# Two-block transformer on one core: the running sums of squares and of the layer norms made by VectorE, not by GpSimd

## The chip, the core and the metric

The kernel runs on one core of a Trainium2 chip. The metric is device time in microseconds (us) of one execution; three runs of the kernel before gave 1494.23, 1493.85 and 1490.75, a median of 1493.85. TensorE (PE) multiplies matrices, VectorE (DVE) and ScalarE (ACT) work elementwise, GpSimd (POOL) does a few elementwise operations here, and SyncE (SP) issues most DMAs. The activations live in SBUF, the products in PSUM; POOL reads and writes SBUF only.

## The reference, cut to what matters

Batch 1, model width D = 1024, 272 tokens (16 meta tokens and 256 of the input). Everything is float32.

```python
def first_block(...):          # two layers
    for i in range(DEPTH):
        a_in = rms_norm(hs, norm_w[i, 0])
        mix = gated_deltanet(a_in, ...) if i % 2 == 0 else mlstm(a_in, ...)
        hs = hs + keep * rms_norm(mix, norm_w[i, 1])
        f = conv_ffn(rms_norm(hs, norm_w[i, 2]), ...)
        hs = hs + keep * rms_norm(f, norm_w[i, 3])
def layer_norm(x, g, b):
    mu = xf.mean(-1, keepdims=True)
    var = jnp.mean(jnp.square(xf - mu), -1, keepdims=True)
    return (xf - mu) * lax.rsqrt(var + LN_EPS) * g + b
def second_block(...):         # two layers: even (convolution, window attention), odd (gated linear, latent attention)
    for layer in range(DEPTH):
        ...
        x = layer_norm(ALPHA * x + y, ln_mix_g[layer], ln_mix_b[layer])
        x = layer_norm(ALPHA * x + swiglu(x, ...), ln_ffn_g[layer], ln_ffn_b[layer])
```

Eight norms close a mixer or a feed-forward: four root-mean-square norms, which need the sum of squares over the width for each token, and four layer norms, which need that and the plain sum.

## The kernel before

The width lies on the partitions: a tile of 128 features by 272 (later 258 or 256) tokens, eight tiles m = 0..7 for the model width. Every product is made of three float32r matmuls, from a high and a low part of each operand (`mm3`, lines 350 to 352; side by side in `group`, lines 373 to 376). The weights stream in chunks of eight 128x128 blocks: SP loads `wraw` (line 318), ACT rounds it to `wh` (line 326), DVE makes the rest `wl` (line 327). There are 413 such chunks.

A sum over the width is taken in two steps. Tiles are added up elementwise into one accumulator tile, and TensorE then sums that tile over the partitions with a matrix of ones. The elementwise adds are what this case is about:

- `post_norm` (line 530) closes the mixers and feed-forwards of the first block and is called four times. Its first loop (lines 540 to 546) takes the eight products of the output projection, squares each on ACT (`sq`, line 543) and adds tiles 0 to 6 up in `acc_sq` (lines 442 to 445): six adds. Its second loop (lines 560 to 574) makes, for each tile m, the scaled product `xn` (line 562, DVE, one input in PSUM), the residual `hs` (line 564, DVE, both inputs in SBUF), a square on ACT (line 572), the high part `xh` on ACT (line 568), the low part `xl` on DVE (line 569, both inputs in SBUF), and again six adds of squares (line 573). The last call has no second sum. `pre_norm` and `group` of the next stage multiply `xh` and `xl` with the first weights as they come; the norm's factor is applied later. Below, the stretches of the first three second loops are called residual stage 1 (at 335 us), 2 (548 us) and 3 (690 us).
- `layer_norm` (line 1216) closes the four sublayers of the second block. It adds tiles 0 to 3 into `ac` (line 1257), sums them on TensorE, subtracts that part of the mean (lines 1269, 1271), then adds tiles 4 to 6 into `ac` (line 1263) and the squares of tiles 0 to 6 into `ac2` (line 1249). Behind the product of tile 7 TensorE sums `ac` and `ac2` (lines 1275, 1276, recorded as line 422) and tile 7 and its square (lines 1282, 1283), and goes on with the raw input `xr` of the next stage (line 1242 on DVE, lines 373 to 376 on TensorE). Below, these are layer norms 1 (at 966 us), 2 (1160 us), 3 (1282 us) and 4 (1440 us, the last). In 1 and 3 a product has K = 8, in 2 and 4 K = 22.

In the trace `ac` and `ac2` are both called `lnacc`, and X and the residual both `hs`.

The order of each engine's instructions is not the order of the code. `IssueOrder` (line 1699) takes all instructions, gives each a fixed duration by engine and shape, and schedules them forwards and backwards in turn over their dependencies; `fix` (line 2024) then holds each engine to the order found. For the adds of this case two of its lines count, with n the elements per partition:

```python
        elif e == DVE:
            t = n * 1.042 + 68 + (60 if len(ins) == 3 else 0)
...
        else:
            t = n * 2.25 + 125
```

The second is POOL's. A duration does not depend on what other engines do at that time.

Of the kernel before, what the change touches and what calls it, by code (L numbers as in the profile page):

```python
# [13 lines left out]
D = 1024  # L14
# [18 lines left out]
# ---------------------------------------------------------------- host layout  # L33
# [40 lines left out]
# the order of the first mixer: projections q (with k), v and z, products and blocks P, inverses D, token-major values and keys T, states S, outputs O  # L74
# [65 lines left out]
def host(inp):  # L140
# [34 lines left out]
    # second block, even layer: head t of kv 0 beside head 4 + t of kv 1  # L175
# [10 lines left out]
    # odd layer  # L186
# [72 lines left out]
# ---------------------------------------------------------------- device  # L259
class Kern:  # L260
# [8 lines left out]
    # ---- helpers  # L269
# [40 lines left out]
    def wload(self, first, need, ahead):  # L310
        """Chunks of weights up to `need`, and `ahead` more as far as the buffers behind `first` go."""
# [27 lines left out]
    def wrow(self):  # L339
        """The next four parts side by side."""  # L340
        ci, j = divmod(self.wpos, CH)
        assert j + 4 <= CH
        for _ in range(4):
            self.wnext()
        return [a[:, j:j + 4].rearrange("p a b -> p (a b)") for a in self.wchunks[ci]]
# [16 lines left out]
    def group(self, items, hook=None):  # L362
        """Several products of K = 8 side by side, so that each part of x serves all of them as it comes."""
# [19 lines left out]
    def halves(self, x, n):  # L383
        """The first four products of K = 16: the last part of x is taken last."""
# [23 lines left out]
    def warm(self, k, ins=None):  # L408
        """Products that nothing reads, behind `ins`, so that the array's clock stays up over a wait."""
# [9 lines left out]
    def stat_cols(self, st, src, n):  # L419
        """Sums over the partitions, one column for each 128 tokens (the last ones overlap)."""  # L420
        for i, s in enumerate(starts(n)):
            r = self.nc.tensor.matmul(st[:, i:i + 1], src[:, s:s + 128], self.ones1, start=True, stop=True)
        return r

    def bcast(self, out, col, n):
        """A column for each 128 tokens to rows on all partitions."""
# [7 lines left out]
    def row_stat(self, acc, sq, n, warm=0):  # L434
        """Sum of squares over all tiles: the running sum and the last tile."""
# [6 lines left out]
    def acc_sq(self, acc, prev, sq, m):  # L442
        """Running sum of the squares of all tiles but the last."""
        if m and m < KD - 1:
            self.nc.gpsimd.tensor_tensor(acc, prev if m == 1 else acc, sq, ALU.add)
# [13 lines left out]
    def rstd(self, st, n, dim, pool, tag="rsy"):  # L459
        """1 / sqrt(st / dim + 1e-6), the same rows on all partitions."""  # L460
# [16 lines left out]
    # ---- norms of the first block  # L477
# [5 lines left out]
    def first_raw(self, pool):  # L483
        """The input of the first mixer, not yet normed, and the columns of its sums of squares."""
# [24 lines left out]
    def pre_norm(self, wname, t0, pool, items, outs, dest=None, st=None, tag="rsy"):  # L509
        """The first products of a stage from its input before the norm, scaled after; then the normed input."""  # L510
# [19 lines left out]
    def post_norm(self, wname, K, x, t0, pool, nxt, tag='mix'):  # L530
        """Output projection, its norm, the residual; then the input of the next stage, not yet normed."""
# [46 lines left out]
    # ---- feed-forward with convolution  # L578
# [38 lines left out]
    # ---- gated delta rule  # L617
    def gdn(self):
# [5 lines left out]
        with ExitStack() as es:  # L624
# [17 lines left out]
            # gates  # L642
# [45 lines left out]
            # cumulative sums and last values  # L688
# [13 lines left out]
            # decay matrices, [j, i]: exponents are the sums of g over j < t <= i  # L702
# [77 lines left out]
    def gdn_blocks(self, g, kq, kq16, E, beta, elg, pool, dpool):  # L780
        """Norms of k, scaled products (attention over E) and the inverses of the diagonal blocks of 16."""
# [9 lines left out]
        # the meta tokens, four heads in slots of 32  # L791
# [3 lines left out]
        # products of keys with keys; the squared norms of the keys on their diagonals  # L795
# [27 lines left out]
        # decayed  # L823
# [3 lines left out]
        # the diagonal blocks of 16, one on a partition  # L827
# [5 lines left out]
        # their inverses by substitution  # L833
# [10 lines left out]
        # products of keys with queries  # L844
# [11 lines left out]
    def gdn_inverse(self, g, X64, Uf, st, pool):  # L856
        """The inverse of the triangular matrix, transposed."""
# [6 lines left out]
        # doubling: blocks of 32, 64 and 128  # L864
# [60 lines left out]
    def gdn_tokens(self, g, kq, v, kq16, v16, st, pool):  # L925
        """Values and keys with the tokens on the partitions, scaled."""
# [29 lines left out]
    def gdn_state(self, g, kq, st, neg, egl, pool):  # L956
        """The states before each chunk; the new values of each chunk take the place of the values."""
# [48 lines left out]
    def gdn_out(self, g, kq, E, st, eg, of, pool):  # L1006
        """The outputs, normed and gated, in place of the gates."""
# [12 lines left out]
        # squared norms of q, one column for each token  # L1020
# [16 lines left out]
        for c in (2, 0, 1):  # L1037
# [16 lines left out]
            # head norm  # L1054
# [21 lines left out]
    # ---- mLSTM  # L1076
# [135 lines left out]
    # ---- second block  # L1212
# [3 lines left out]
    def layer_norm(self, name, K, x, pool, last=False, tags=("xr0", "xr1", "xr2", "xr3")):  # L1216
# [11 lines left out]
        if not last:  # L1228
            # the input of the next stage, not yet normed; beside it the gain and the offset as columns
# [14 lines left out]
        def square(m):  # L1244
# [3 lines left out]
            if 1 <= m < KD - 1:  # L1248
                GP.tensor_tensor(ac2, prev if m == 1 else ac2, sq, add)
            prev = sq  # L1250

        for m in range(KD):
            ps = self.proj(K, x, n)
            if m < 4:
                V.scalar_tensor_tensor(X[:, m], X[:, m], ALPHA, ps, mult, add)
                if m:
                    GP.tensor_tensor(ac, X[:, 0] if m == 1 else ac, X[:, m], add)
            else:
# [3 lines left out]
                if 4 < m < KD - 1:  # L1262
                    GP.tensor_tensor(ac, X[:, 4] if m == 5 else ac, X[:, m], add)
# [48 lines left out]
    def norm_product(self, i, raw, pool, out=None, scale=1.0):  # L1312
        """A product of an input before the layer norm: without its offset, and the offset; or all of it."""
# [33 lines left out]
    def softmax(self, pool, sbank, tag, scale, mask, sink, vT, out, tp=None):  # L1347
        """sbank: scores [query, (256 keys of block 1 | 128 keys of block 0)], out: [dv, 256 queries]."""
# [81 lines left out]
    def odd(self, xf):  # L1430
# [5 lines left out]
        with tc.tile_pool(name="op", bufs=1, reuse_waits="tile") as pool:  # L1436
# [18 lines left out]
            # gates of the linear attention, rotary key, queries and keys  # L1455
# [22 lines left out]
            # linear attention: decayed products, level by level  # L1478
# [44 lines left out]
            # latent attention: queries, keys, values  # L1523
# [118 lines left out]
    # ---- whole program  # L1642
# [410 lines left out]
```

## Time and profile before

| | |
|---|---|
| three runs, us | 1490.75, 1493.85, 1494.23 |
| profiled execution: span, us | 1496.2 |
| busy: PE, DVE, ACT, POOL | 97%, 71%, 56%, 13% |
| chain that ended last, by engine | PE 86%, DVE 6%, DMA, POOL and issue 2% each, ACT 1% |
| HBM traffic | 148 GB/s over the span |
| POOL adds of lines 445, 1249, 1257, 1263 | 42, 24, 12 and 8, 86 of POOL's 286 instructions |

The time of the profiled execution is its span, 1496.2 us, 2.4 us over the median of the three runs. A busy share counts an engine as busy while an instruction is on it, also when that runs slowly. The chain that ended last is followed back from the last instruction; PE's share is the time in which it was PE's own work that the end waited for. The granted clock of PE is 1.00 at the higher of its two levels (2.4 GHz) and 0.50 at the lower (1.2 GHz); values between are means over a stretch.

### The profile page before, as it was taken

To read this page: it belongs to the slowest core of one execution; us is meant where nothing else is said; L and a number is where in the kernel's file an instruction comes from. 1 tells how busy PE (TensorE), PEld (TensorE's weight loads), DVE (VectorE), ACT (ScalarE), POOL (GpSimd) and SP (SyncE) were. 2 spreads that over 40 slices of the span, in tenths; PEclk is the share of its full clock that TensorE was granted. 3 is DMA by queue.
4 is the path that set the end of the run, shared out by engine and by line. 5 is a ranking of instruction groups with operands and counts; after the bars stand their busy time and mean duration, and the time that the engine had idled before them with its cause. 6 is when DMAs were issued, how large, how long until landed. Compare 5 with 4: busy or idle time off the path is not lost.

```text
span 1496.2 us, 30607 instructions
## 1 busy us (share of the span) xinstructions
PE 1456.1 (97%) x12258; PEld 1403.7 (94%) x12258; DVE 1056.8 (71%) x1976; ACT 842.9 (56%) x1560; POOL 188.4 (13%) x286
## 2 busy tenths in 40 slices
PE   8899999999999999999999999999999999999997
PEld 7898998998999989889999998999999978999997
DVE  8996585548988357657988456686556798875553
ACT  5456565546766446446766446565444666654442
POOL 3472032121000120003000000020001200300011
PEclk9999998999999999999999999989999999999999
DMA  4343422354655534323665543537555424375551
GB/s 161 103 132 103 150 81 62 112 171 147 215 171 180 172 127 157 119 78 119 206 197 179 189 155 113 176 107 222 187 182 183 144 72 155 128 220 188 182 186 57
DMA packets 72670, 223.96 MB, mean 150 GB/s; under 512 B 16784, under 2 KB 18896, under 8 KB 72400
## 3 DMA queue, kind: packets, MB, share of 16 engines
q1 hardware_dynamic: 71952, 220.38, 45.5%
q8 instruction: 96, 1.57, 0.4%
q10 hardware_dynamic: 576, 1.62, 0.3%
q14 instruction: 46, 0.38, 0.1%
HBM read 220.34 MB, written 1.64 MB: 148 GB/s over the span
## 4 chain that ended last, share of the span: by engine, by line
PE 86%; DVE 6%; DMA 2%; POOL 2%; issue 2%; ACT 1%; SPq 0%; DVEq 0%; ACTq 0%; POOLq 0%
PE acc L352 17%; PE acc L350 17%; PE acc L351 17%; PE psa L350 3%; PE psa L352 3%; PE psa L351 3%; PE psb L351 2%; PE psb L352 2%; PE psb L350 2%; PE acc L376 1%; PE acc L373 1%; PE acc L374 1%; DVE wl L327 1%; POOL Xb L842 1%; DVE hs L564 1%
## 5 line engine op out<-in xcount | busy, mean ns | idle before, releaser
L327 DVE TENSOR_TENSOR wl<-wraw,wh 128x1024 fp32r<-128x1024 f32 x413 | 508.1, 1233 | 228.2 <-ACT wh L326 226.8
L326 ACT ACTIVATE wh<-wraw 128x1024 fp32r<-128x1024 f32 x413 | 435.2, 1056 | 277.8 <-PE acc L351 154.9
L352 PE MATMUL acc<-xh,wl 128*128 128x256 f32 (+1 forms) x848 | 246.7, 291 | 1.2 <-DVE wl L327 1.2
L350 PE MATMUL acc<-xh,wh 128*128 128x256 f32 (+1 forms) x848 | 245.5, 290 | 1.0 <-DVE kq L727 1.0
L351 PE MATMUL acc<-xl,wh 128*128 128x256 f32 (+1 forms) x848 | 245.6, 290 | 0.7 <-issue 0.7
L350 PE MATMUL acc<-ah,wh 128*128 128x256 f32 (+1 forms) x704 | 198.0, 283 | 0.0
L351 PE MATMUL acc<-al,wh 128*128 128x256 f32 (+1 forms) x704 | 197.9, 282 | 0.0
L352 PE MATMUL acc<-ah,wl 128*128 128x256 f32 (+1 forms) x704 | 196.7, 282 | 0.0
L352 PEld LDWEIGHTS acc<-xh,wl 128*128 128x128 f32 x848 | 161.5, 191 | 4.3 <-issue 1.7
L350 PEld LDWEIGHTS acc<-xh,wh 128*128 128x128 f32 x848 | 161.3, 190 | 2.4 <-ACT wh L326 1.2
L351 PEld LDWEIGHTS acc<-xl,wh 128*128 128x128 f32 x848 | 161.1, 190 | 1.5 <-issue 0.9
L350 PEld LDWEIGHTS acc<-ah,wh 128*128 128x128 f32 x704 | 132.5, 189 | 0.1
L351 PEld LDWEIGHTS acc<-al,wh 128*128 128x128 f32 x704 | 132.5, 189 | 0.1
L352 PEld LDWEIGHTS acc<-ah,wl 128*128 128x128 f32 x704 | 131.9, 188 | 0.0
L352 PE MATMUL acc<-xnh,wl 128*128 128x272 f32 (+1 forms) x424 | 122.2, 288 | 0.0
L350 PE MATMUL acc<-xnh,wh 128*128 128x272 f32 (+1 forms) x424 | 122.0, 288 | 0.0
L351 PE MATMUL acc<-xnl,wh 128*128 128x272 f32 (+1 forms) x424 | 121.9, 287 | 0.0
L352 PE MATMUL acc<-oh,wl 128*128 128x256 f32 (+2 forms) x304 | 86.4, 286 | 0.5 <-DVE wl L327 0.5
L351 PE MATMUL acc<-ol,wh 128*128 128x256 f32 (+2 forms) x304 | 86.1, 285 | 0.1
L350 PE MATMUL acc<-oh,wh 128*128 128x256 f32 (+2 forms) x304 | 85.2, 286 | 0.0
L350 PEld LDWEIGHTS acc<-xnh,wh 128*128 128x128 f32 x424 | 79.8, 188 | 1.5 <-issue 1.3
L352 PEld LDWEIGHTS acc<-xnh,wl 128*128 128x128 f32 x424 | 79.8, 188 | 1.4 <-issue 1.2
(715 smaller groups left out, 3483.8 us busy)
## 6 DMA issues: line engine op xcount, KB each, us to landing
wraw<-in_w_dram SPq DMA_DIRECT2D x413, 512.0 KB, 3.4
late<-in_late_dram ACTq DMA_DIRECT2D x1, 1206.5 KB, 5.7
hs<-in_x_dram SPq DMA_DIRECT2D x4, 272.0 KB
out_dram<-hs SPq DMA_DIRECT2D x8, 128.0 KB, 1.9
d<-PT SPq DMA_DIRECT2D x32, 9.0 KB, 1.5
cst<-in_cst_dram SPq DMA_DIRECT2D x1, 339.5 KB
A<-d SPq DMA_DIRECT2D x4, 72.0 KB
d<-Xb SPq DMA_DIRECT2D x4, 72.0 KB
```

Source lines behind the costliest of these rows:

```text
L326: nc.scalar.activation(h, raw, AF.Copy)
L327: nc.vector.tensor_tensor(l, raw, h.bitcast(F32), ALU.subtract)
L350: mm(ps, h, xh, start=start, stop=False)
L351: mm(ps, h, xl, start=False, stop=False)
L352: mm(ps, l, xh, start=False, stop=stop)
L373: mm(o, h, x(k)[0], start=k == 0, stop=False)
L374: mm(o, l, x(k)[0], start=False, stop=False)
L376: mm(o, w[k][0][:, :m], x(k)[1], start=False, stop=k == KD - 1)
L564: V.tensor_tensor(hs, hs, t, ALU.add)
L842: GP.tensor_tensor(Xb[:, j + 1:16, 0:m], Xb[:, j + 1:16, 0:m], tv, sub)
```

## The change

Four lines get another engine. Nothing is added or left out, and the operands stay.

```diff
     def acc_sq(self, acc, prev, sq, m):
         if m and m < KD - 1:
-            self.nc.gpsimd.tensor_tensor(acc, prev if m == 1 else acc, sq, ALU.add)
+            self.nc.vector.tensor_tensor(acc, prev if m == 1 else acc, sq, ALU.add)
...
             if 1 <= m < KD - 1:
-                GP.tensor_tensor(ac2, prev if m == 1 else ac2, sq, add)
+                V.tensor_tensor(ac2, prev if m == 1 else ac2, sq, add)
...
                 if m:
-                    GP.tensor_tensor(ac, X[:, 0] if m == 1 else ac, X[:, m], add)
+                    V.tensor_tensor(ac, X[:, 0] if m == 1 else ac, X[:, m], add)
...
                 if 4 < m < KD - 1:
-                    GP.tensor_tensor(ac, X[:, 4] if m == 5 else ac, X[:, m], add)
+                    V.tensor_tensor(ac, X[:, 4] if m == 5 else ac, X[:, m], add)
```

The diff also drops comments. Since the scheduler knows the engine and the duration of each instruction, it makes a new order for all engines from the first of these adds on (at about 300 us of the trace); before it the order is the same. POOL keeps the small powers (lines 555, 1288) and its part in the first mixer. SP's order is the same.

DVE in layer norm 1, before: from the subtraction of the first part of the mean (lines 1271, 1269) to the first use of the sums (line 1277). `xr` is the low part of the raw input, `wl` a chunk of weights.

```order
L1271 TENSOR_TENSOR hs<-hs,lnpc 128x256 x4
L1269 SCALAR_TENSOR_TENSOR hs<-hs,lnpc 128x256 x3
L1259 TENSOR_TENSOR hs<-hs,acc 128x256
L1269 SCALAR_TENSOR_TENSOR hs<-hs,lnpc 128x256
L1259 TENSOR_TENSOR hs<-hs,acc 128x256
L1242 SCALAR_TENSOR_TENSOR xr<-hs,late,xr 128x256 x4
L327 TENSOR_TENSOR wl<-wraw,wh 128x1024
L1259 TENSOR_TENSOR hs<-hs,acc 128x256
L1242 SCALAR_TENSOR_TENSOR xr<-hs,late,xr 128x256 x2
L327 TENSOR_TENSOR wl<-wraw,wh 128x1024
L1259 TENSOR_TENSOR hs<-hs,acc 128x256
L1277 TENSOR_SCALAR lnp_11941<-psb_11940 128x2
```

The same place in the changed kernel, from tile 5 on. Ahead of these rows stand the eight subtractions, one `xr`, tile 4, another `xr` and three adds of squares.

```order
L1259 TENSOR_TENSOR hs<-hs,acc 128x256
L1249 TENSOR_TENSOR lnacc_11938<-lnacc_11938,lnsq 128x256
L1242 SCALAR_TENSOR_TENSOR xr<-hs,late,xr 128x256
L1263 TENSOR_TENSOR lnacc<-hs 128x256
L1259 TENSOR_TENSOR hs<-hs,acc 128x256
L1249 TENSOR_TENSOR lnacc_11938<-lnacc_11938,lnsq 128x256
L1263 TENSOR_TENSOR lnacc<-lnacc,hs 128x256
L1242 SCALAR_TENSOR_TENSOR xr<-hs,late,xr 128x256
L1249 TENSOR_TENSOR lnacc_11938<-lnacc_11938,lnsq 128x256
L327 TENSOR_TENSOR wl<-wraw,wh 128x1024
L1259 TENSOR_TENSOR hs<-hs,acc 128x256
L1277 TENSOR_SCALAR lnp_11941<-psb_11940 128x2
```

Tile 6 (the third line-1259 row of the kernel before, the second here) and the two sums now stand ahead of the chunk of weights that stood ahead of tile 6, and the fourth `xr` now stands behind the last add into `ac`.

DVE in residual stage 3, before, from the second `xl` to the last ones:

```order
L569 SCALAR_TENSOR_TENSOR xl<-hs,par,xh 128x258
L564 TENSOR_TENSOR hs<-hs,xn 128x258
L562 TENSOR_TENSOR xn<-mix,st 128x258
L564 TENSOR_TENSOR hs<-hs,xn 128x258
L562 TENSOR_TENSOR xn<-mix,st 128x258
L569 SCALAR_TENSOR_TENSOR xl<-hs,par,xh 128x258
L564 TENSOR_TENSOR hs<-hs,xn 128x258
L562 TENSOR_TENSOR xn<-mix,st 128x258
L564 TENSOR_TENSOR hs<-hs,xn 128x258
L569 SCALAR_TENSOR_TENSOR xl<-hs,par,xh 128x258 x5
```

In the changed kernel the first three `xl` stand close together, and the other five behind the last add (`acc`); these are the rows from the fifth `xn` on:

```order
L562 TENSOR_TENSOR xn<-mix,st 128x258 x2
L445 TENSOR_TENSOR acc<-acc,sq 128x258
L564 TENSOR_TENSOR hs<-hs,xn 128x258 x2
L562 TENSOR_TENSOR xn<-mix,st 128x258
L445 TENSOR_TENSOR acc<-acc,sq 128x258
L564 TENSOR_TENSOR hs<-hs,xn 128x258
L562 TENSOR_TENSOR xn<-mix,st 128x258
L445 TENSOR_TENSOR acc<-acc,sq 128x258
L564 TENSOR_TENSOR hs<-hs,xn 128x258
L445 TENSOR_TENSOR acc<-acc,sq 128x258
L569 SCALAR_TENSOR_TENSOR xl<-hs,par,xh 128x258 x4
```

Between the third and the fourth `xl` DVE now has 15 other instructions, where it had three.

## Rows read from the trace of the kernel before

**Rows 1.** The page's first part: busy time, share of the span, instructions.
```profile
PE 1456.1 (97%) x12258; PEld 1403.7 (94%) x12258; DVE 1056.8 (71%) x1976; ACT 842.9 (56%) x1560; POOL 188.4 (13%) x286
```

**Rows 2.** Stretches: length; PE, PEld, DVE, ACT, POOL busy; PEclk, DMA share, GB/s.
```profile
335.00:350.00 15.00, 12.74 (x79) 11.23 (x78) 12.62 (x27) 8.88 (x20) 5.21 (x6) 0.89 0.08 31
...
548.00:562.00 14.00, 12.12 (x92) 10.96 (x93) 12.75 (x28) 8.72 (x19) 5.46 (x7) 1.00 0.12 39
...
690.00:705.00 15.00, 13.11 (x98) 12.19 (x99) 13.64 (x28) 8.38 (x19) 5.25 (x7) 1.00 0.22 70
...
966.00:990.00 24.00, 21.97 (x162) 21.71 (x161) 20.70 (x36) 13.06 (x24) 10.48 (x12) 0.87 0.46 140
990.00:1005.00 15.00, 15.00 (x113) 15.00 (x112) 11.06 (x29) 9.64 (x27) 0.28 (x1) 0.86 0.17 61
...
1285.00:1300.00 15.00, 13.54 (x99) 13.05 (x98) 13.13 (x24) 7.82 (x16) 7.40 (x8) 0.89 0.34 116
```

**Rows 3.** Waits of PE over the span: us in total, times, longest us.
```profile
PE acc L376 <- DVE xl L569: 3.2, 6, 1.3
...
PE psb L422 <- POOL lnacc L1263: 2.6, 2, 2.0
...
PE psa L376 <- DVE xl L569: 1.0, 2, 0.8
...
PE psa L422 <- DVE hs L1259: 0.8, 1, 0.8
```

**Rows 4.** DVE groups, shapes apart: count; busy us, mean ns; idle before.
```profile
L564 DVE TENSOR_TENSOR hs<-hs,xn 128x272 f32<-128x272 f32 x16 | 9.5, 623 | 0.0
L569 DVE SCALAR_TENSOR_TENSOR xl<-hs,par,xh 128x272 fp32r<-128x272 f32 x16 | 8.8, 595 | 0.0
...
L562 DVE TENSOR_TENSOR xn<-mix,st 128x272 f32<-128x272 f32 x16 | 6.4, 429 | 3.3 <-PE st L430 3.3
...
L564 DVE TENSOR_TENSOR hs<-hs,xn 128x256 f32<-128x256 f32 x8 | 3.1, 417 | 0.0
```

**Rows 5.** A POOL group, same columns.
```profile
L445 POOL TENSOR_TENSOR acc<-acc,sq 128x272 f32<-128x272 f32 x20 | 19.0, 951 | 55.2 <-ACT sq L543 51.4 <-ACT sq L572 3.3
```

**Rows 6.** Timeline of DVE in residual stage 1: start us, us; equal neighbours merged (x2).
```profile
335.20 0.78 DVE L562 TENSOR_TENSOR xn<-mix,st 128x272 f32<-128x272 f32 x2 [1.65 <-PE st L430]
335.91 0.79 DVE L564 TENSOR_TENSOR hs<-hs,xn 128x272 f32<-128x272 f32 x2
...
344.91 1.73 DVE L569 SCALAR_TENSOR_TENSOR xl<-hs,par,xh 128x272 fp32r<-128x272 f32 x4
```

**Rows 7.** Timeline of residual stage 3: DVE's first, one `xl`, PE's sum of squares.
```profile
691.33 0.76 DVE L562 TENSOR_TENSOR xn<-mix,st 128x258 f32<-128x258 f32 x2 [0.49 <-PE st L430]
...
693.37 0.49 DVE L569 SCALAR_TENSOR_TENSOR xl<-hs,par,xh 128x258 fp32r<-128x258 f32 x1
...
701.77 0.60 PE L406 MATMUL st<-acc,ones 128*128 128x258 f32 x2
```

**Rows 8.** Timeline of layer norm 1: DVE, POOL and PE at the sums.
```profile
973.51 1.43 DVE L1271 TENSOR_TENSOR hs<-hs,lnpc 128x256 f32<-128x256 f32 x4
...
981.54 1.21 DVE L327 TENSOR_TENSOR wl<-wraw,wh 128x1024 fp32r<-128x1024 f32 x1
982.67 0.41 DVE L1259 TENSOR_TENSOR hs<-hs,acc 128x256 f32<-128x256 f32 x1
...
983.23 0.84 POOL L1263 TENSOR_TENSOR lnacc<-lnacc,hs 128x256 f32<-128x256 f32 x1 [1.89 <-DVE hs L1259]
...
984.12 1.01 PE L422 MATMUL psb<-ones,lnacc 128*128 128x1 f32 x4 [2.03 <-POOL lnacc L1263]
```

**Rows 9.** Stretches of 4 us in layer norm 1, columns as in rows 2.
```profile
960.00:964.00 4.00, 4.00 (x36) 4.00 (x35) 1.71 (x3) 0.53 (x3) 0.00 (x0) 1.00 0.59 194
...
984.00:988.00 4.00, 3.88 (x19) 3.88 (x19) 3.61 (x6) 2.50 (x5) 0.93 (x2) 0.50 0.53 170
```

**Rows 10.** The odd mixer, columns as in rows 2.
```profile
1195.00:1275.00 80.00, 77.41 (x559) 66.63 (x558) 72.19 (x167) 53.51 (x112) 1.62 (x2) 0.96 0.36 117
```

## The prediction

> **What bounds the kernel now.** I began with the page's busy line: PE is at work for 97% of the span, with about 40 us idle in all [rows 1]. So the end is set by PE, and taking 86 adds from POOL and giving them to DVE is worth nothing by itself. What counts is where PE waits, and how fast it runs. The table of waits comes next. Over the whole span PE waits 4.2 us for `xl` of line 569, 2.6 us (twice) for a POOL add of line 1263 and 0.8 us for the `hs` of line 1259 [rows 3]. All of these lie in residual stages and layer norms, where the moved adds are.
>
> Then I cut these places into stretches [rows 2]. In the three residual stages PE is idle for 2.26, 1.88 and 1.89 us, while DVE is busy for 12.62 of 15, 12.75 of 14 and 13.64 of 15: DVE paces them. In stage 1 the mean clock is 0.89, a loss of 15 x 0.11 = 1.65 us. In layer norm 1 it is 0.87 and 0.86 in two stretches on end, although PE does not idle at all in the second. That is the lower level: 19 matmuls in 4 us, against 36 in 4 us twenty microseconds earlier [rows 9].
>
> Last, the shapes one by one show why DVE is so full. The same residual add of line 564 takes 623 ns where POOL adds beside it, and 417 ns, on 256 columns and not 272, in the last `post_norm`, which has no second sum; `xn` of line 562, with one input in PSUM, takes 429 ns in both kinds of company [rows 4]. POOL's adds need 951 ns in the mean [rows 5]. So the adds are not free for DVE today: its instructions with both inputs in SBUF are stretched while POOL works.
>
> **What an add costs on DVE.** No such add runs on DVE before, so I take it from its likes. Two undisturbed line-562 instructions take 0.78 us together, and the next group starts 0.71 us after the first, 0.355 each [rows 6]. Four undisturbed adds of 256 columns take 1.43 us, of which the last has 0.42, so 0.335 each [rows 8]. The low parts `xl` follow each other at (1.73 - 0.49) / 3 = 0.41, where one undisturbed takes 0.49 [rows 6, 7]. The bounds are 0.335 and, if the stretch stayed, 0.62.
>
> **Residual stages.** In stage 1 DVE makes 24 instructions in 335.20 to 346.64, 11.44 us [rows 6]. Afterwards it makes 22 at 0.355 and 8 `xl` at 0.41, 11.1 us. So the six adds (2.1 us) are paid by the stretch that goes: 8 x (0.623 - 0.417) = 1.65 for `hs` and 8 x (0.595 - 0.49) = 0.84 for `xl` [rows 4, 7], 2.5 together. What PE waited longest for here is the fifth `xl` (the first of the last four), done at 345.4; in the new order 21 instructions and five `xl` are done by 335.20 + 7.46 + 2.05 = 344.7. I take 0.5. The slower clock there I leave as it is. Stage 2 has the same counts in an order that suits PE no better: -0.2. In stage 3 the last add ends at 691.33 + 22 x 0.355 + 3 x 0.41 = 700.4, so PE can sum the squares at 700.6 and not at 701.77 [rows 7]. But the fourth `xl` now comes after it, at about the time it had before. I take 1.0 of the 1.2 us. Sum **1.3 us**, between -1.5 (the new order makes PE wait for `xl` in each) and +4 (stage 1 also gets its clock back).
>
> Weighed against this is a rule of the Trainium skill ("Perfetto Trace Analysis", section "Optimizing Scalar/DVE Operations"): where DVE is saturated, offloading some of its work to ScalarE or even GpSimd may make sense. That speaks for the kernel before, since DVE is the full engine in these stages, and by it the stages would lose time. The same passage adds that GpSimd and DVE share a read port of SBUF, so that moving work between those two might not help. The rows with 623 and 417 ns agree with the second sentence, and by that one the stages come out about even, as my sum has it. If only the first held, the second rival below would be the result.
>
> **Layer norm 1.** PE ends its products at about 982.1 and waits 2.03 us for POOL's last `lnacc` [rows 8]. The chain before that is on DVE: tile 6 is drained at 982.67, behind a `wl` of 1.21 us. Afterwards that `wl` stands behind the adds. DVE makes 21 instructions from 973.51 to the last add into `ac`: at 0.335 that is 980.6, and two more bring `ac2` to 981.3, before PE's products end. I leave 0.4 for the signal: gain 1.6.
>
> With the wait goes, I think, the slow spell behind it. The clock was 1.00 until that wait; the spell cost 24 x 0.13 + 15 x 0.14 = 5.2 us [rows 2]. Layer norms 2 and 4 make the same one-column sums without such a wait, and no row shows PE waiting on POOL there [rows 3]. I take 5.1 back. Some is returned: DVE still has a chunk of weights (1.21) to make ahead of the variance, and at full clock PE arrives sooner. I put that at 1.2, between 0 and 3. Sum 1.6 + 5.1 - 1.2 = **5.5**; bounds 0 and 7.
>
> **Layer norm 3.** It is built the same way. PE is idle for 1.46 us in 1285 to 1300, of which 2.6 - 2.0 = 0.6 is the second wait for `lnacc` and 0.8 the one for `hs` [rows 2, 3]. The clock of 0.89 costs 1.65. I take 1.2 + 1.65 and return 0.25: **2.6**, bounds 0 and 3.1.
>
> **What I cost at nothing.** The 24 adds of the four first loops: POOL idled 51.4 us before them waiting for ACT's squares [rows 5], so they come one at a time with the products, and DVE, 71% busy in all [rows 1], has gaps for them. If that cover were gone, one add of 0.355 would lie on the path four times, 1.4 us. Layer norms 2 and 4: a tile has 66 matmuls at 4/36 us, 7.3 us, against an add of 0.335; without cover 0.7 us together. SP's queue does not move, so no transfer is issued earlier by order. The scheduler also reshuffles places without moved adds, the odd mixer above all; PE idles 2.6 of 80 us there, and the clock of 0.96 costs 3.2 [rows 10]. I enter 0, within 3 either way.
>
> **Sum.** 1.3 + 5.5 + 2.6 = 9.4 us. The profiled execution (1496.2) would become 1486.8. It lies 2.4 over the median; measured from the median, 1493.85 - 9.4 = **1484.5 us**.
>
> **The rivals.** *The clock falls all the same.* If the one-column sums, or the short idling around them, are enough to lower it, only the waits go: 1.3 + 1.6 + 0.95 = 3.9 us, so 1490.0, no change that can be told. For it: stage 1 and the odd mixer show lower clocks too [rows 2, 10]. Against it: in layer norm 1 the spell begins with the 2 us wait, and stages 2 and 3 idle 1.9 us at a clock of 1.00. Chance 0.18.
>
> *VectorE becomes the bound.* If the stretch has another cause than POOL (ACT's traffic, say), each stage pays 6 x 0.355 = 2.1 us in full, 6.4 for three, and each of layer norms 1 and 3 pays 8 x 0.335 = 2.7 less POOL's last add of 0.84, 3.7 for both, with the clock as it was: 10.1 us slower, **1504**. It decides from the point where the relief per stage is under 2.1 us, that is, where line 564 stays above about 0.47 us with `xl` back at 0.49. Against it stands the pair 623 and 417 ns [rows 4]. Chance 0.06.
>
> *The new order loses elsewhere.* One more slow spell or a stall like the 2.6 us of the odd mixer, in two or three places, takes back what the layer norms give: 6 us or more lost there, so 1490 to 1497. Chance 0.10.
>
> **How the numbers follow.** My forecast has the remaining 0.66. About 0.3%, 4.5 us, is what a measurement of this kernel can tell from no change, so "same" is 1489.4 to 1498.3. The low end takes the better bounds together: stage 1 with its clock 1.65, nothing returned in layer norm 1 1.2, the rest of the reorder 2.5: about 1479. The high end takes the first rival with the reorder 3 to 4 us against it: 1494. Faster 0.70 (the forecast, and a little of the third rival), same 0.21, slower 0.09.
>
> **What the profile of the changed kernel would show.** POOL with 86 instructions fewer; line 564 at 272 columns back at about 0.42 to 0.45 us and line 569 near 0.49; the adds on DVE near 0.42 each. DVE's busy time up by clearly less than 86 x 0.42 = 36 us. No wait of PE for a POOL `lnacc`. A clock of 1.00 through layer norm 1, with about 7 us fewer between its first subtraction and the next products on normed input. I am wrong if the clock falls there without the wait, if line 564 stays near 0.6, or if the even or odd mixer grows by more than 3 us.

## The result and the profile after

The changed kernel takes 1487.45 us in the median of six runs, against 1494.04 for six of the kernel before: a ratio of 0.9941 (95% interval 0.9924 to 0.9959), 6.6 us by the medians. A second comparison gave 0.9962 (0.9948 to 0.9977). So the time lies inside the forecast's range and the sign is right; the gain is some 6 to 7 us where 9.4 were forecast.

The busy line of the changed kernel's page:

```profile
PE 1443.0 (98%) x12258; PEld 1393.6 (94%) x12258; DVE 1067.9 (72%) x2062; ACT 842.7 (57%) x1560; POOL 104.8 (7%) x200
```

Its waits of PE over the span (us in total, times, longest):

```profile
PE psa L430 <- POOL lnv L1288: 2.9, 3, 1.8
...
PE acc L376 <- DVE xl L569: 1.7, 2, 1.4
PE psa L376 <- DVE xl L569: 1.6, 1, 1.6
```

Its groups of DVE with the shapes apart, columns as in rows 4:

```profile
L445 DVE TENSOR_TENSOR acc<-acc,sq 128x272 f32<-128x272 f32 x20 | 8.7, 435 | 2.7 <-ACT sq L543 2.6
L1249 DVE TENSOR_TENSOR lnacc<-lnacc,lnsq 128x256 f32<-128x256 f32 x20 | 8.4, 419 | 0.5
L569 DVE SCALAR_TENSOR_TENSOR xl<-hs,par,xh 128x272 fp32r<-128x272 f32 x16 | 7.5, 495 | 0.0
L564 DVE TENSOR_TENSOR hs<-hs,xn 128x272 f32<-128x272 f32 x16 | 6.7, 432 | 0.0
L562 DVE TENSOR_TENSOR xn<-mix,st 128x272 f32<-128x272 f32 x16 | 6.5, 429 | 3.3 <-PE st L430 3.3
```

POOL has 86 instructions fewer. DVE makes 86 more and is busy only 11.1 us longer, though they last 0.42 to 0.44 us each: line 564 went from 623 to 432 ns and line 569 from 595 to 495, while line 562 stayed [rows 4]. The waits for `lnacc` and for the `hs` of line 1259 [rows 3] are gone, and the wait for `lnv`, POOL's small power of line 1288, now leads the table with 2.9 us; before, PE waited 0.4 us for it, once, in the last layer norm.

The stretches of rows 2 and 9, at the same places of the program (earlier on the time axis, since time has been saved), columns as in rows 2:

```profile
328.00:343.00 15.00, 13.30 (x97) 12.41 (x97) 14.20 (x35) 11.11 (x22) 0.00 (x0) 1.00 0.11 36
...
679.00:694.00 15.00, 13.80 (x111) 13.26 (x110) 14.19 (x36) 8.96 (x20) 1.48 (x1) 1.00 0.23 80
955.00:979.00 24.00, 23.47 (x198) 23.21 (x197) 21.15 (x51) 13.78 (x27) 2.00 (x1) 1.00 0.47 147
979.00:994.00 15.00, 15.00 (x129) 15.00 (x129) 14.08 (x34) 11.23 (x30) 0.00 (x0) 1.00 0.33 118
1268.00:1283.00 15.00, 13.18 (x113) 12.98 (x112) 12.63 (x34) 8.74 (x20) 2.98 (x1) 1.00 0.28 92
```

The column that changed most is the clock, third from the end: 0.87 and 0.86 in layer norm 1, 0.89 in layer norm 3 and in residual stage 1 [rows 2] are all 1.00 now. In the second stretch of layer norm 1 PE gets 129 matmuls done where it got 113.

The timeline of layer norm 1 in the changed kernel, DVE's last adds into the two accumulators:

```profile
968.77 0.42 DVE L1263 TENSOR_TENSOR lnacc<-lnacc,hs 128x256 f32<-128x256 f32 x1
...
969.50 0.42 DVE L1249 TENSOR_TENSOR lnacc<-lnacc,lnsq 128x256 f32<-128x256 f32 x1
```

PE's sums of them in the same timeline:

```profile
970.55 0.95 PE L422 MATMUL psb<-ones,lnacc 128*128 128x1 f32 x8
```

POOL's power in layer norms 1 and 3, from the timeline of POOL:

```profile
974.89 2.00 POOL L1288 TENSOR_TENSOR lnv<-lnv,fst 128x2 f32<-128x2 f32 x1 [98.33 <-DVE lnv L1287]
...
1277.12 2.98 POOL L1288 TENSOR_TENSOR lnv<-lnv,fst 128x2 f32<-128x2 f32 x1 [89.92 <-DVE lnv L1287]
```

And PE behind the power in layer norm 1:

```profile
976.95 0.71 PE L430 MATMUL psa<-fst,lnv 128*128 128x128 f32 x4 [0.53 <-POOL lnv L1288]
```

The same power before, in layer norms 1 and 3:

```profile
989.41 0.87 POOL L1288 TENSOR_TENSOR lnv<-lnv,fst 128x2 f32<-128x2 f32 x1 [4.48 <-DVE lnv L1287]
...
1295.49 0.87 POOL L1288 TENSOR_TENSOR lnv<-lnv,fst 128x2 f32<-128x2 f32 x1 [3.80 <-DVE lnv L1287]
```

Both sums are complete at 969.9, before PE's products end at 970.55, and PE passes to them without idling; before, it stood still for 2.03 us [rows 8]. But the power behind them took 0.87 us before and takes 2.00 in layer norm 1 and 2.98 in layer norm 3 now, and PE waits for it, 0.53 and 1.82 us.

**One execution against many.** The profiled execution of the changed kernel is its fastest (1480.4), and its span is 18.0 us under that of before. Of these, 7.3 us lie ahead of residual stage 1, nearly all in code that is the same: before, the clock was at its lower level from 236.5 to 250.1 us, in this execution it was not, and in the next one it was again. So I compare stretches from profiles, and totals from all executions. For each of these the span and the mean granted clock are known. In the table, span x (1 - clock) stands for what the clock took: it is what the lower clock costs if PE sets the pace wherever the clock is low.

| mean per execution, us | executions | span | taken by the clock | the rest |
|---|---|---|---|---|
| kernel before | 57 | 1492.5 | 20.0 | 1472.6 |
| changed kernel | 12 | 1485.5 | 15.2 | 1470.3 |

By this account 4.7 of the 7.0 us gained are clock and 2.3 waits and work. But the account does not measure the cost, and by these figures it makes the clock's part too large. Among the 57 executions of the kernel before the column "taken" spreads more than the span (standard deviations 2.2 and 1.5 us), and a straight line through them gives 0.56 us of span for each us taken. The two profiles of the changed kernel have 10.2 us and no lower clock at all in the odd mixer, and between layer norms 2 and 3 they differ by 0.4 us (132.6 and 132.2 in the table of stretches below); with no lower clock PE is idle there for 4.8 of 80 us, with it for 2.6. How the 7.0 us divide is not shown by these columns.

The spans also put right a figure from ahead of the prediction, where the span of 1496.2 us was taken for the time of its execution. In each of the 151 executions for which both are known the time is 1.7 to 2.4 us longer than the span, so that execution lay about 4 us over the median and not 2.4.

### The profile page after: what moved, and what is told of

Read it like the earlier page. It is cut to its first block, busy times and chain, and to the rows that moved or that the text cites. A ratio compares the mean times of both kernels' runs of the same rounds, so it can differ in the third digit from the quotient of the medians.

```text
span 1478.2 us, 30530 instructions
## 1 busy us (share of the span) xinstructions
PE 1443.0 (98%) x12258; PEld 1393.6 (94%) x12258; DVE 1067.9 (72%) x2062; ACT 842.7 (57%) x1560; POOL 104.8 (7%) x200
## 4 chain that ended last, share of the span: by engine, by line
PE 85%; DVE 8%; POOL 3%; ACT 2%; DMA 2%; issue 1%; SPq 0%; POOLq 0%; DVEq 0%; ACTq 0%
PE acc L352 18%; PE acc L350 18%; PE acc L351 18%; PE psa L350 3%; PE psa L352 3%; PE psa L351 3%; PE psb L352 2%; PE psb L350 2%; PE psb L351 2%; DVE wl L327 1%; PE acc L376 1%; PE acc L373 1%; PE acc L374 1%; POOL Xb L842 1%; DMA wraw<-in_w_dram 1%
## 5 line engine op out<-in xcount | busy, mean ns | idle before, releaser
L350 PEld LDWEIGHTS acc<-ah,wh 128*128 128x128 f32 x704 | 132.6, 189 | 0.1
```

The source lines that it names most:

```text
L350: mm(ps, h, xh, start=start, stop=False)
```

## The experiments

Eleven runs were made, of the two kernels again and of eight others. Ratios are to the kernel before, run on the same chip. Where the place matters, this table gives the length in us between DVE's first instructions of one stage and the next: residual stages (line 562) and the first of the eight subtractions of layer norms 1 to 4 (line 1269 or 1271); the odd mixer is counted with layer norm 2.

| kernel | start to stage 1 | stage 1 to 2 | 2 to 3 | 3 to last `post_norm` | to layer norm 1 | 1 to 2 | 2 to 3 | 3 to 4 |
|---|---|---|---|---|---|---|---|---|
| before | 335.2 | 213.8 | 142.3 | 197.7 | 84.4 | 177.3 | 131.3 | 173.2 |
| before_again | 334.2 | 213.6 | 142.3 | 197.7 | 84.7 | 177.3 | 131.3 | 173.2 |
| changed | 327.9 | 211.6 | 141.8 | 196.0 | 84.5 | 171.1 | 132.6 | 171.4 |
| after_again | 335.8 | 213.1 | 142.4 | 196.0 | 85.1 | 170.9 | 132.2 | 171.4 |
| ln_only | 334.0 | 213.5 | 142.3 | 197.7 | 84.3 | 171.2 | 130.3 | 172.9 |
| res_only | 336.5 | 211.7 | 142.2 | 196.0 | 84.4 | 176.1 | 132.8 | 173.0 |
| both_add | 334.6 | 215.3 | 145.7 | 197.8 | 85.0 | 176.2 | 133.0 | 174.4 |
| before_warm2 | 332.8 | 212.1 | 142.3 | 197.7 | 84.7 | 173.7 | 133.4 | 172.4 |
| power_again | 334.7 | 211.8 | 141.8 | 196.0 | 83.5 | 170.9 | 130.7 | 169.9 |

### The same two kernels again

before_again and after_again have no edit.

> The kernel before, once more, for a second profile. Theory A (the fall of the clock at the sums of layer norms 1 and 3 belongs to PE's wait for POOL's lnacc): the waits of about 2.0 and 0.6 us are there again and the clock falls to the lower level in the same two places, 3.4 us or more of it behind the long wait; first subtraction of layer norm 1 to first subtraction of line 1300 takes 20 to 22 us. Theory B (the falls come by chance, as the one at 236 us did that only one of the two first profiles shows): the wait is there, the clock is 1.00 behind it, and that stretch takes 16 to 17 us. Both: ratio 1.00.

> The changed kernel, once more. Theory A: layer norm 1 takes 14 us from the first subtraction to the first one of line 1300, clock 1.00 there; ratio 0.993 to 0.997. Theory B: falls of the clock somewhere else or here with the same likelihood as before, and the gain of the median, 6.6 us, is the waits (some 3 to 4 us from residual stage 1 to the end) and luck: ratio 0.996 to 0.999.

before_again: ratio 0.9998 (0.9989 to 1.0007). Its profile has the waits of 2.33 and 0.59 us for `lnacc`, and the lower clock for 10.2 us from the end of the first wait on and for 3.4 us in layer norm 3, both lengths to a tenth of a microsecond as in the first profile. after_again: 0.9962, no lower clock in either place. The rival, falls by chance, is out for these two places; for the one at 236 us chance it is.

### One part of the change at a time

ln_only leaves line 445 as it was, res_only leaves lines 1249, 1257 and 1263:

```diff
 ln_only
-            self.nc.vector.tensor_tensor(acc, prev if m == 1 else acc, sq, ALU.add)
+            self.nc.gpsimd.tensor_tensor(acc, prev if m == 1 else acc, sq, ALU.add)
 res_only
-                V.tensor_tensor(ac2, prev if m == 1 else ac2, sq, add)
+                GP.tensor_tensor(ac2, prev if m == 1 else ac2, sq, add)
...
```

> Only the adds of the layer norms (lines 1249, 1257, 1263) are on DVE; line 445 stays on POOL. Theory A (most of the gain is layer norms 1 and 3, wait and clock): 5 to 9 us faster than before, layer norm 1 at 14 us, line 564 at 0.62 us still. Theory B: 2 to 3 us faster. Theory C (the gain comes from the end of the contention in the residual stages): no more than 1 us.

> Only line 445 is on DVE; the layer norms' adds stay on POOL. Theory A: 1 to 3 us faster than before, line 564 at 0.43 us, layer norm 1 as before (wait of 2 us, slow clock behind it). Theory C: 4 to 6 us faster.

ln_only: 1488.96 us, ratio 0.9958 (0.9944 to 0.9971), as much as the whole change on the same chip (1488.60). res_only: 1493.39, 0.9995 (0.9984 to 1.0005), under the 1 to 3 us expected. The gain is the layer norms'. Yet line 564 is at 436 ns in res_only, and its stretches to stage 2 and behind stage 3 are 2.1 and 1.8 us shorter. Up to 1.7 of the 2.1 are the 3.4 us at the lower clock at 346 us, which come and go with line 445 on either engine: before_warm, with its adds on POOL, does not have them, after_again, with its adds on DVE, has them at 360 us. What happened to the rest shows, by the same account, in the means of its 12 executions: the rest is 1469.1, 3.5 under the kernel before, and the clock takes 22.4, 2.4 more. Why the clock takes more there I can't say; its profile has a lower clock in the odd mixer for 10.2 us, against 6.8 before.

### What the contention costs

In both_add DVE makes the real adds and POOL makes each once more, into a tile that nothing reads:

```diff
+    def idle_add(self, a, b):
+        o = self.small.tile([128, T1], F32, name="idle")[:, :a.shape[-1]]
+        self.nc.gpsimd.tensor_tensor(o, a, b, ALU.add)
...
             self.nc.vector.tensor_tensor(acc, prev if m == 1 else acc, sq, ALU.add)
+            self.idle_add(prev, sq)
```

> The changed kernel, and POOL makes each of the 86 adds once more, into a tile that nothing reads; PE waits for DVE's adds alone. Theory A (POOL's adds stretch DVE's instructions with two inputs in SBUF): line 564 is back at 0.6 us or over, line 1269 at about 0.65, each residual stage 2 us or more longer than in the changed kernel, layer norms 1 and 3 longer by 2 to 5 us with the clock lower behind the sums; 8 to 16 us slower than the changed kernel, so ratio to the kernel before 1.001 to 1.007. Rival (the stretch has another cause than POOL, or costs nothing): line 564 stays at 0.43 us and the time that of the changed kernel, ratio 0.995 to 0.997.

1503.96 us, ratio 1.0062 (1.0048 to 1.0076): by the ratios 15 us slower than after_again (1.0062 - 0.9962 of 1494), and 18 against the first comparison. So POOL's adds cost that, with the new order that they bring, although no one waits for their results: DVE's own adds come later by them, PE waits 2.8 us for DVE's `lnacc`, and the clock falls behind that (table below). They lengthen the DVE instructions with two inputs in SBUF that meet them, and these are others than in the kernel before: line 564 (here 569) is at 483 and 520 ns and not at the 600 I expected, the subtractions of line 1269 at 448 and not at 650, but `xl` is at 661 and the adds themselves are at 659. `xn`, with one input in PSUM, stays at 427. The timeline of residual stage 1 shows how. POOL's adds in both_add:

```profile
336.73 0.99 POOL L444 TENSOR_TENSOR idle<-sq 128x272 f32<-128x272 f32 x1 [3.10 <-ACT sq L577]
338.62 0.86 POOL L444 TENSOR_TENSOR idle<-sq 128x272 f32<-128x272 f32 x1 [0.90 <-ACT sq L577]
340.39 0.77 POOL L444 TENSOR_TENSOR idle<-sq 128x272 f32<-128x272 f32 x1 [0.90 <-ACT sq L577]
```

DVE in the same stretch (line 449 makes `acc`, 567 `xn`, 569 `hs`, 574 `xl`):

```profile
337.01 1.01 DVE L449 TENSOR_TENSOR acc<-sq 128x272 f32<-128x272 f32 x1
337.94 0.90 DVE L574 SCALAR_TENSOR_TENSOR xl<-hs,par,xh 128x272 fp32r<-128x272 f32 x2
338.77 1.02 DVE L569 TENSOR_TENSOR hs<-hs,xn 128x272 f32<-128x272 f32 x1
339.70 0.43 DVE L449 TENSOR_TENSOR acc<-acc,sq 128x272 f32<-128x272 f32 x1
340.06 0.42 DVE L567 TENSOR_TENSOR xn<-mix,st 128x272 f32<-128x272 f32 x1
340.40 1.04 DVE L574 SCALAR_TENSOR_TENSOR xl<-hs,par,xh 128x272 fp32r<-128x272 f32 x1
```

Each of the three DVE instructions that starts under a POOL add ends 0.28 to 0.31 us after that add does: 338.02 after 337.72, 339.79 after 339.48, 341.44 after 341.16. The one behind the second, away from POOL, takes 0.43. So an instruction is held until POOL is through, or nearly, and then runs; it is not slowed in proportion. The whole trace of both_add bears this out: 58 DVE instructions of 256 to 272 columns with two inputs in SBUF start under one of POOL's added adds and outlast it, and all end 0.28 to 0.31 us after it; 13 `wl` of 1024 columns, which take 1.2 us alone, end 1.08 or 1.09 us after it. (Seven more started under an add as POOL's record has it and took their own 0.41 to 0.43; there the add, at 1.02 to 1.43 us, was the one that was held up.) The Trainium skill ("SBUF — State Buffer", section "Who interferes with whom") states that a DVE instruction with two SBUF inputs contends with a GpSimd instruction that reads SBUF, and calls the shared port pair an exclusive lock, with the order of issue deciding who blocks. These rows agree.

### What lowers the clock in the layer norms

Three kernels set the wait and the adds apart. last_on_pool gives POOL back the last add into each accumulator in layer norms 1 to 3. before_warm is the kernel before with nine products that nothing reads between tile 7 and the first sums in layer norms 1 and 3, before_warm2 has six more ahead of the sums of tile 7. In both, further lines, not shown, hold the sums behind the added products:

```diff
 last_on_pool, lines 1249 and 1263
-                V.tensor_tensor(ac2, prev if m == 1 else ac2, sq, add)
+                (GP if m == KD - 2 and not last else V).tensor_tensor(ac2, prev if m == 1 else ac2, sq, add)
...
 before_warm
-            if m == KD - 2:
+            if m == (KD - 1 if K == KD else KD - 2):
+                if K == KD:
+                    self.warm(9, self.last_pe())
...
 before_warm2, further
+                if K == KD:
+                    self.warm(6, self.last_pe())
```

> The changed kernel with the last add into each of the two accumulators of layer norms 1, 2 and 3 back on POOL: 6 of 86 adds. Theory A (one late POOL add is what PE waits for, and the clock falls behind that wait): if PE waits 1 us or more for lnacc in layer norm 1, the clock falls there and half or more of the 6.5 us goes; if the wait is under 0.6 us, the clock stays up and the time is that of the changed kernel within 2 us. Rival (the clock falls with the contention of all the adds, or by chance): no fall even with a wait of 1 us or more, or a fall without one.

> The kernel before, with nine products that nothing reads (128 columns, float32) on PE between the last product of tile 7 and the sums, in layer norms 1 and 3. The adds stay on POOL, so the wait for lnacc stays, but PE is not idle in it. Theory A (the lower clock comes from PE idling in the wait): the clock is 1.00 through layer norms 1 and 3, layer norm 1 takes 16 to 17 us and not 21.4, layer norm 3 is 1 to 2 us shorter, ratio 0.995 to 0.997. Rival (the one-column sums or the contention lower the clock, not the idling): it falls as before, ratio 0.999 to 1.002.

> As before_warm, and six more products that nothing reads between the sums of the two accumulators and those of tile 7, so that PE is not idle in the wait for tile 7 either (0.8 us in both layer norms of before_warm). POOL still makes the adds. Theory A (idling beside the one-column sums is what the fall follows): no lower clock within 10 us of the sums of layer norms 1 and 3, layer norm 1 takes 17 to 18 us and layer norm 3 15 to 16 by the subtraction's first to line 1300's first; ratio 0.995 to 0.998. Rival (POOL's adds, or the one-column sums alone): the clock falls in at least one of the two, as in before_warm; ratio 0.998 to 1.000.

last_on_pool: ratio 0.9957 (0.9943 to 0.9971), from five executions; a sixth took 6693.57 us and is left out, its cause unknown. before_warm: 0.9988 (0.9977 to 0.9998), less than expected, and its clock fell: the 2 us wait was filled, but the next wait came up, for tile 7. The timeline of PE at the sums of tile 7 in last_on_pool, layer norms 1 and 3:

```profile
978.95 0.61 PE L422 MATMUL psa<-ones,hs 128*128 128x1 f32 x4 [0.75 <-DVE hs L1259]
...
1282.76 0.61 PE L422 MATMUL psa<-ones,hs 128*128 128x1 f32 x4 [0.40 <-DVE hs L1259]
```

The same in before_warm, layer norm 1, from the first sums on (its lines 427 and 1264 are 422 and 1259 of before):

```profile
982.45 0.98 PE L427 MATMUL psb<-ones,lnacc 128*128 128x1 f32 x8
984.23 0.61 PE L427 MATMUL psa<-ones,hs 128*128 128x1 f32 x4 [0.81 <-DVE hs L1264]
```

before_warm2 fills that one too. The stretch of 11 us around the sums of layer norm 1, columns as in rows 2, first in before:

```profile
984.00:995.00 11.00, 10.88 (x54) 10.88 (x55) 6.26 (x14) 3.08 (x6) 1.80 (x3) 0.53 0.57 187
```

The same in before_warm:

```profile
980.00:991.00 11.00, 10.19 (x76) 10.11 (x75) 7.92 (x16) 4.33 (x8) 2.41 (x3) 0.84 0.59 191
```

And in before_warm2:

```profile
978.00:989.00 11.00, 11.00 (x97) 11.00 (x96) 9.08 (x19) 5.52 (x11) 2.80 (x3) 1.00 0.61 192
```

With POOL still adding (2.80 us of it in the stretch) and the same one-column sums, the clock stays at its higher level once PE does not idle. It is the clock that speaks for theory A here, not the time: before_warm2 runs at 0.9982 (0.9970 to 0.9995), short of the 0.995 to 0.998 expected and inside the rival's range, and layer norm 3 takes 16.6 us where 15 to 16 were expected (layer norm 1 17.4). In the table of stretches 1 to 2 and 3 to 4 are 3.6 and 0.8 us shorter than before, with the waits filled and not removed. So the clock alone is worth about that much of the 6.2 and 1.8 us that the changed kernel gains there, as far as the new order has no part in it. But the stretch with the odd mixer is 2.1 us longer in its new order, with 10.2 us at the lower clock in it against 6.8. In the mean of the 12 executions the account gives 14.0 us taken by the clock against 20.0, and 3.2 more for the rest, the added products among it. All profiles together, in us, idle time of PE from the end of tile 7's products to the last sum, and the lower clock at or behind it:

| kernel | layer norm 1: idle, lower clock | layer norm 3: idle, lower clock |
|---|---|---|
| before | 2.03, 10.2 | 0.62 + 0.80, 3.4 |
| before_again | 2.33, 10.2 | 0.59 + 0.80, 3.4 |
| res_only | 1.80, 6.8 | 0.44 + 0.80, 3.4 |
| both_add | 1.51 + 0.27 + 0.87, 6.8 | 1.26 + 0.31, 6.8 |
| before_warm | 0.81, 3.4 | 0.05 + 0.80, 6.8 |
| last_on_pool | 0.75, 3.4 | 0.40, 3.4 |
| before_warm2 | 0, none | 0, none |
| changed, after_again, ln_only, power_cost, power_again, ln_power | 0, none | 0, none |

Twelve places with idling ahead of or between the one-column sums, twelve falls; fourteen without, no fall there. (ln_only has a fall of 3.4 us some 5 us behind the sums of layer norm 3, right after a wait of 1.84 us for `lnv`; the changed kernel and after_again wait 1.82 us in that place without a fall.) Layer norm 2 makes the same sums without idling, and none of the 13 profiles has a lower clock within 10 us of them. Whether the one-column sums have a part in it is not shown. In the two profiles of the kernel before the fall of layer norm 1 begins 0.1 and 0.2 us ahead of the first sum, when PE has idled for 1.9 and 2.1 us.

My condition in last_on_pool was put on the wrong wait. PE does not wait for `lnacc` there at all; it idles for tile 7, 0.75 and 0.40 us, and the clock falls all the same, in both layer norms. That is the rival's case as I had worded it, a fall without the wait for `lnacc`. Yet the time is that of the changed kernel, as I had it for a clock that stays up: two falls of 3.4 us did not show in it.

### What the new wait costs

power_cost is the changed kernel with one number of the scheduler changed, so that the power's two columns count for 2.03 us and not 0.63; power_again repeats it, and ln_power is power_cost with line 445 back on POOL:

```diff
-            t = n * 165 + 300
+            t = n * 165 + (1700 if n == 2 else 300)
```

> The changed kernel with one number of the scheduler's durations changed: POOL's power of two columns (line 1288) is taken for 2.0 us, as the changed kernel's trace has it in layer norm 1, and not for 0.6. The scheduler then puts the variance (line 1287) ahead of a chunk of weights. Theory A (what layer norms 1 and 3 still lose is this power, which DVE's work beside it delays): PE's wait for lnv shrinks by 0.5 to 1.5 us in all, ratio to the kernel before 0.994 to 0.996. Rival (the new order only moves the loss): the time of the changed kernel, or up to 2 us slower.

> power_cost once more, beside ln_power on one chip: ratio to the kernel before 0.991 to 0.994, no lower clock behind the sums of layer norms 1 and 3.

> power_cost with the adds of line 445 back on POOL: only the layer norms' adds are on DVE. If the residual stages' adds are worth what their traces show (2 to 4 us of PE's time), it is 2 to 4 us slower than power_cost. If they are worth nothing in the median, as res_only and ln_only against the changed kernel suggest, it is within 1.5 us of it.

power_cost: 1483.86 us, 0.9924 (0.9911 to 0.9938); power_again: 1482.91, 0.9923 (0.9911 to 0.9935). That beats both kernels, 10 to 11 us under the one before and 3 to 6 (by the ratios) under the changed one, more than expected. POOL's power in the timeline of power_again, layer norms 1 and 3:

```profile
980.19 0.87 POOL L1288 TENSOR_TENSOR lnv<-lnv,fst 128x2 f32<-128x2 f32 x1 [96.69 <-DVE lnv L1287]
...
1282.29 1.91 POOL L1288 TENSOR_TENSOR lnv<-lnv,fst 128x2 f32<-128x2 f32 x1 [88.98 <-DVE lnv L1287]
```

It is back at 0.87 in layer norm 1 and shorter, 1.91, in layer norm 3, and PE waits 0.5 us for it in all instead of 2.9. In the table of stretches 3 to 4 gained 1.5 us by that. 2 to 3 is 1.5 to 1.9 shorter as well, and the one ahead of layer norm 1 by 1.0 to 1.6; no power that PE waits for lies there, so that part of the gain is the new order's luck. ln_power: 1485.35, 0.9940 (0.9928 to 0.9952), 2.4 us slower than power_again: here the residual stages' adds are worth what their traces promise. In res_only they were worth 0.8, and ln_only without them was as fast as the whole change, so their worth lies between nothing and 2.4 us and hangs on the rest of the kernel.

## Why the prediction was right in its sign, and where it was too large

**The price of an add and the relief.** Right. The 30 DVE instructions of stage 1 were put at 11.1 us; they run from 327.95 to 339.05. Line 564 was put at 0.42 to 0.45 and line 569 at 0.49: 0.432 and 0.495. One reading said more than its row: that `xn` takes 429 ns "in both kinds of company". Rows 4 have it beside POOL's adds alone; in the last `post_norm` the trace has 413, on 256 columns, which fits. The rule of the Trainium skill that a full DVE may hand work to GpSimd ("Perfetto Trace Analysis", section "Optimizing Scalar/DVE Operations") points the wrong way here. DVE was busy only 11.1 us longer with adds of some 36 us, so on POOL they took from DVE about 25 of the 36 us that they saved it. The sentence behind it in the Trainium skill, that the two engines share an SBUF read port and moving work between them might not help, is the one that agrees with these numbers.

**Residual stages, 1.3 us.** The places were right, the sum in the profiles is larger: 2.2 (with 1.7 of clock) or 0.8 to stage 2, 0.5 or -0.2 to stage 3, and 1.8 behind it, where I had taken 1.0. The working for stage 1 misread one row. PE's longest wait there, 1.35 us, was for the fourth `xl` and not for the fifth:

```profile
343.42 0.64 DVE L569 SCALAR_TENSOR_TENSOR xl<-hs,par,xh 128x272 fp32r<-128x272 f32 x1
...
344.12 0.39 PE L376 MATMUL acc<-xl,wh 128*128 128x272 f32 x1 [1.35 <-DVE xl L569]
```

For the fifth it waited 0.18 us. In the changed kernel it is the fifth, done 9.51 us after the stage's first instruction as forecast, and PE waits 1.4 us for it. In stage 2 the longest wait for `xl` grew from 0.8 to 1.6 us, and in stage 3 the two of 0.5 are gone. In the median of res_only 0.8 are left of all this; by the account above the clock took the rest back.

**Layer norm 1, 5.5 us, and layer norm 3, 2.6.** Measured from one subtraction to the next: 6.2 and 6.4 us, and 1.8 twice. Wait and clock went together, as said. I had 1.2 us returned because a chunk of weights stands ahead of the variance; what was returned is POOL's power, held up by DVE's instructions, 0.53 us in layer norm 1 and 1.82 in 3. The place was right, the mechanism was not: I had the contention as POOL holding up DVE, and left out that DVE holds up POOL too. In layer norm 3 the 0.25 us that I returned were the term that was too small, and with it the 2.6 came out too large.

**What I set at 0.** The reordered stretches are not quite 0: the one with the odd mixer is 0.9 to 1.3 us longer, the one ahead of layer norm 1 0.1 to 0.4, within the 3 I had allowed. The 6 us of the third rival did not come.

**From one execution to the median.** This is the step that was too large. I took the whole 9.4 us from one profile and subtracted them from the median. For profiled executions the sum was good: from residual stage 1 to the end the two pairs of profiles differ by 10.7 and 8.5 us. But that execution lost 23.9 us to the clock by the account (1496.2 x 0.016), where 57 executions lose 20.0 in the mean, and the changed kernel's 12 lose 15.2. So the clock's part is 4.7 and not the 6.75 that I had from the profile, and waits and work gave 2.3 where 4.1 less 1.45 returned, 2.65, were forecast: 7.0 and not 9.4. How the 7.0 us divide into the two parts is as uncertain as the account. What does not hang on it is that the profiled execution was longer than most, with a span of 1496.2 us against a mean of 1492.5, and had more to gain. That the sum fits the two pairs of profiles owes something to luck, for its terms missed in both directions.

**The rivals.** The clock did not fall all the same: in these layer norms it fell where PE idled at the sums, and nowhere else but in the one place of ln_only. VectorE did not become the bound. That both_add comes to the 1504 of that rival is chance: there POOL is the cause after all, and a lower clock has its part.

## What to carry to other kernels

When two engines share a path, count an instruction's cost on both: 86 adds moved to the fuller engine cost it 11 us of busy time and not 36, because the emptier engine had been holding it up. Look where TensorE idles at the sums of a norm, for waits of 0.4 to 2.3 us there were followed by 3 to 10 us at the lower clock in twelve places of twelve. Take a clock's cost from many executions, not from the one that was profiled, and from the lengths of stretches with and without it: in the odd mixer two profiles of one kernel, with 10.2 us of it and with none, differ by 0.4 us.

## What the runs showed of the hardware that I had not expected

The contention works in both directions. DVE under a POOL add ended 0.28 to 0.31 us after that add. POOL's power of two columns, 0.69 us undisturbed (the last layer norm of the changed kernel), took 0.80 to 2.99 us in the 13 profiles where it began under a DVE instruction with two SBUF inputs. The timeline of DVE in layer norm 3 of the changed kernel, where the power ran from 1277.12 to 1280.10:

```profile
1276.87 2.35 DVE L327 TENSOR_TENSOR wl<-wraw,wh 128x1024 fp32r<-128x1024 f32 x2
1279.14 0.41 DVE L1300 TENSOR_TENSOR hs<-hs,lnacc 128x256 f32<-128x256 f32 x1
1279.47 0.48 DVE L1242 SCALAR_TENSOR_TENSOR xr<-hs,late,xr 128x256 fp32r<-128x256 f32 x1
```

The power ends 0.55 us after the instruction of line 1300, which ends at 1279.55. So it is in every such place: the power ended 0.55 or 0.56 us after a DVE instruction of this kind, but not always after the first. In layer norms 1 and 3 of the kernel before it was the first that met it (0.87 us), in layer norm 1 of the changed kernel the second (2.00), here the third (2.98). What decides that stays open. It is not a gap, for DVE ran without one where the power took 0.87, and in layer norm 1 of power_again (0.87) the same two instructions, an `xr` and a `wl`, met it at the same distance as in the changed kernel (2.00).

Idling of 0.40 us among sixteen one-column products was followed by 3.4 us at the lower clock, and 0.8 us by 3.4 in one place and 6.8 in another; what decides the length stays open. So does why the clock takes 2.4 us more in res_only than before.
